# Expert rows and activations transposed by VectorE in blocks of 32, weights stored in the order of the chunks, rows gathered a quarter per partition

## The chip, the cores and the metric

The kernel runs on one core of one Trainium2 chip. The metric is the device time of one execution in microseconds (us). Five engines work beside each other, each through its own list of instructions in order: TensorE (PE; PEld is its loading of weights), VectorE (DVE), ScalarE (ACT), GpSimd (POOL) and SyncE (SP, which here only issues transfers). Sixteen DMA engines move data between the memory (HBM) and the on-chip buffer (SBUF, 128 partitions); they are fed by queues, q1 for the transfers that SP issues and q0 for those of POOL. Products end in PSUM, eight banks.

## The reference

512 tokens of 1024 features pass through two blocks. Block 1: a norm, a mixer of pools and attention, an output product, a residual, and then a layer of 32 experts of which each token takes four:

```python
def moe(h, w_router, b_router, w_gate_up, b_gate_up, w_down, b_down):
    logits = (ht @ w_router + b_router).astype(jnp.float32)
    top_vals, top_idx = lax.top_k(logits, TOP_K)           # 4 of 32
    gates = jax.nn.softmax(top_vals, axis=-1)
    ...
    def expert_block(args):
        xblk, e = args
        gu = xblk @ w_gate_up[e] + b_gate_up[e]             # 1024 x 2048
        gate = jnp.minimum(gu[:, :D_EXPERT], SWIGLU_LIMIT)
        up = jnp.clip(gu[:, D_EXPERT:], -SWIGLU_LIMIT, SWIGLU_LIMIT)
        act = gate * jax.nn.sigmoid(SWIGLU_ALPHA * gate) * (up + 1)
        return act @ w_down[e] + b_down[e]                  # 1024 x 1024
    ...
    y = jnp.zeros((T + 1, D), h.dtype).at[row_tok].add(row_gate[:, None].astype(h.dtype) * yb)
```

Block 2 holds a gated delta rule beside a sparse attention, an output product, a norm and a gate. All is computed in float32. The 32 experts hold 12.58 MB of weights each, 403 MB in all.

## The kernel before

**Stages.** Block 1 up to the router takes about the first 240 us, the experts run to about 1306 us, block 2 from there to the end. Only the experts and the seams on both sides are touched.

**The stream of weights.** An expert is six chunks of 2 MB: four of gate and up (256 rows of the contraction each, `load_q`, line 382) and two of down (512 rows each, line 388). A chunk lies in SBUF as 128 partitions of 16 KB. Of gate and up a partition gets two rows of 8 KB, of down four rows of 4 KB. The 192 chunks go in one order into a ring of slots (nine in steady use, `PAT`); SP issues a chunk as soon as the products that read its slot are done (`more`). Chunks 7 to 9 are issued on POOL's queue. SP also loads the biases (`bias`, lines 1115 and 1116).

**The order of the experts.** After the first two they run by a plan by rank of load: `expert_plan` gives each of the 32 places room for 2, 3 or 4 groups of 32 rows, 86 groups together. Which expert stands at a place is known only at run time (`perm`). Rows beyond the room are done in a loop at the end, which has no turns here.

**One expert, in the order of the code** (the loop over `i`). Gate and up: for each of eight steps `kc` of the contraction and each group four products (`gate_up`, L1140), each of 32 rows against 128 x 512 weights, into a bank of PSUM. Beside them the next experts are made ready:

- `prep_a(i + 2)`: products with a one-hot matrix give the token numbers, gates and rates of the rows (L416, L417); then POOL gathers the rows from `h_rows` (`gather`, L404), whole rows of 4 KB, one row per partition, 64 to 128 rows.
- `prep_r(i + 2)`: one product (L441) brings token numbers, gates and rates into the layout of the products (`iy`, `gt`, `rs`).
- `prep_b(i + 1)`: eight transposes by TensorE (L1128, tile `pht`) and two products by VectorE out of PSUM with the gain of the norm (L1129) make `hT`, the rows by feature; a shuffle spreads the biases (L1133).

Then for each group `act` on VectorE and ScalarE (L1146 to L1154), `act_t` with two transposes by TensorE (L1160, tile `pat`) and a copy by ScalarE (L1162), and `down` with 32 products (L1171), the bias and the gate on VectorE (L1176, L1177) and a scatter by POOL that adds the rows to `y_rows` (L1179), 128 rows of 1 KB. The transposes of the last group stand inside the down products of the group before it, since the in-order TensorE would wait for `act` otherwise.

**The seams.** For expert 0 the token numbers come by a path of their own (`place_0`, `rows_0`, L1040, then L1057 and one gather), so that its first product can start early. At the last expert POOL issues the first weights of block 2 (`load_w2`, L454, L455 and L463), and its last down chunk comes in two halves.

Of the kernel before, what the change touches and what calls it, by code (L numbers as in the profile page):

```python
# [24 lines left out]
# ---------------------------------------------------------------- packed columns  # L25
# [10 lines left out]
for _n, _w in (("ident", 128), ("g_attn", 8), ("tri", 128), ("cmask", 128), ("iota", 128), ("invrow", 16), ("invcol", 1),  # L36
               ("sgncol", 1), ("poolfix", 64), ("pcol", 1), ("pcol4", 1), ("jcol", 1), ("dumr", 1), ("sel", 128), ("grp", 4), ("kadd", 1), ("caps", 32), ("eye4", 32),
               ("g_q_a", 2), ("g_kv_a", 1), ("b_pool", 4), ("pool_scale", 4),
               ("g_out_pool", 4), ("g_out_attn", 4), ("g_ffn", 8), ("c", 8), ("b_ada", 16), ("g_pre", 8)):
    _col(_n, _w)  # L40
# [77 lines left out]

def layout(inputs):
# [10 lines left out]
    pk["g_ffn"] = col(f("g_ffn_norm"))  # L130
    pk["c"] = col(f("c_2"))
# [3 lines left out]
    for n, (o, w) in _COLS.items():  # L135
# [45 lines left out]
        "w_gu": f("w_gate_up")[0],  # L181
        "w_dn": f("w_down")[0],
# [15 lines left out]
def expert_plan():  # L198
    """Order in which the experts run (by rank of load; ranks 0 and 1 are experts 0 and 1) and groups of 32 rows for each."""
# [14 lines left out]
class Model:  # L214
    """When the engines, each in its order, would be through with the instructions given so far (in us)."""
# [75 lines left out]
def build(tc, ia, out, dbg=None):  # L291
# [12 lines left out]
    with ctx:  # L304
# [10 lines left out]
        hdram = nc.dram_tensor("h_rows", (513, 1024), F32).ap()  # L315
# [27 lines left out]
        # ============================================================ block 1, before the experts  # L343
# [10 lines left out]
        ig0 = mid.tile([128, 1], I32, name="ig0")  # L354
# [4 lines left out]
        # ---- expert weights: one stream of chunks over the rings  # L359
# [19 lines left out]
        def load_q(i, q, e, key, eng=S):  # L379
            w = rings[key].tile([128, 4096], F32, name="ew", tag=key)  # L380
            if q < 4:
                eng.dma_start(w.rearrange("p (k n) -> p k n", k=2),
                            ia["w_gu"][e, 256 * q:256 * q + 256, :].rearrange("o (k p) n -> p (o k) n", p=128))
            else:
                # the very last one in two, so that half of it is used while the other comes
                m = 2 if (i, q) == chunks[-1] else 4
                for k in range(0, 4, m):
                    r = 512 * (q - 4) + 128 * k
                    eng.dma_start(w.rearrange("p (k n) -> p k n", k=4)[:, k:k + m],
                                  ia["w_dn"][e, r:r + 128 * m, :].rearrange("o (k p) n -> p (o k) n", p=128))  # L390
            loaded[i, q] = w

        # ---- rows of the experts
# [42 lines left out]
        def prep_r(i, bank):  # L436
            """Rows, gates and rates in the layout of the products."""
# [6 lines left out]
            V.tensor_scalar(iy[:, :ng], pv[:, :, 0], C("jcol"), None, op0=add)  # L444
            V.tensor_copy(gt[:, :ng], pv[:, :, 1])
# [19 lines left out]
        with tc.tile_pool(name="t1", bufs=1) as tp, tc.tile_pool(name="ps1", bufs=1, space=PSUM) as ps:  # L465
# [5 lines left out]
            # ---- loads, in the order of their use  # L471
# [52 lines left out]
            # ---- rms norm of x, transposed  # L524
# [15 lines left out]
            # ---- latent projections by tokens  # L540
# [27 lines left out]
            # ---- rope tables; those of the queries carry the scale of the scores  # L568
# [51 lines left out]
            # ---- rel_bias of block 2 by distance: row 128 h + 127 - q has the distances of the query q, descending  # L620
# [11 lines left out]
            # ---- pool mixer, a group at a time  # L632
# [48 lines left out]
            # ---- modulation sums  # L681
# [34 lines left out]
            def mod_cols(q):  # L716
                """Shift and scale, by rows."""
# [24 lines left out]
            # ---- heads  # L742
# [19 lines left out]
            # ---- attention  # L762
# [55 lines left out]
            # ---- order of the work  # L818
# [9 lines left out]
            S.dma_start(hdram[512:513].rearrange("o (p n) -> (o p) n", p=128), zt[:, :8])  # L828
# [100 lines left out]
            # ---- output projection, residual, router  # L929
# [99 lines left out]
            oh0 = tp.tile([128, 4, 128], BF, name="oh0")  # L1029
            pk = [pmm(), pmm(), pmm()]  # L1030

            def place_0(t):
                """The rows of expert 0 in a tile, by their place: the first expert wins a tie, so its mask is a comparison."""
                src = pk[t // 3][:, t % 3:t % 3 + 1]
                V.tensor_scalar(oh0[:, t, :n0], C("iota")[:, :n0], src, m0f[:, t:t + 1], op0=ALU.is_equal, op1=mul)
# [21 lines left out]
            V.tensor_scalar(ig0[:n0], pk[2][:n0, :1], 2048.0, 0.25, op0=add, op1=mul)  # L1057
# [8 lines left out]
            # the rates of the rows in three exact parts  # L1066
# [12 lines left out]
        # ============================================================ experts  # L1079
        with tc.tile_pool(name="mo", bufs=1) as mp, \  # L1080
# [13 lines left out]
            bank = lambda name: ps.tile([128, 512], F32, name=name, tag="a", bufs=5)  # L1094
            bank2 = lambda name: ps.tile([128, 512], F32, name=name, tag="b", bufs=2)

            # the slot of the first chunk, in pieces of the tiles of the products
# [21 lines left out]
            def prep_b(i, hf):  # L1119
                """The rows, transposed; the biases, in all rows."""  # L1120
                st = ST[i]
                n = st["n"]
                if hf == 0:
                    st["hT"] = mp.tile([128, 8, 128], F32, name="hT2", bufs=2)
                p = bank2("pht").rearrange("p (c n) -> p c n", c=4)
# [1074 lines left out]
```

## Time and profile before

| | |
|---|---|
| median of 3 runs | 1701.57 us (1700.75 to 1701.81) |
| the profiled execution: its span, first to last instruction | 1702.8 us |
| TensorE busy | 1583.6 us, 93% |
| VectorE busy | 813.9 us, 48% |
| ScalarE busy | 322.7 us, 19% |
| POOL busy | 285.2 us, 17% |
| moved by DMA | 489.86 MB, mean 288 GB/s |

The profile gives no time for its execution other than the span; the span is 1.2 us above the median of the runs. "Busy" is the time in which an engine executes something; on TensorE it holds a slower clock and the small gaps inside a run of products as well. A DMA share is the mean over 16 engines of the time in which packets were under way; at the edges of packets it counts a little twice, so that it can pass 1. "Landing" is the time from a transfer's issue to its end. In names, `ew` is a chunk of the experts' weights, `hg` the gathered rows, `hT` the transposed rows, `pgu` and `pdn` the sums of gate and up and of down, `zt` a piece of one slot that holds the activations and the results, `cpk` the packed constants.

### The profile page before, as it was taken

The numbers are of one execution on the slowest core, as the hardware profiler recorded it, in microseconds if no ns is written. First come the engines' busy times: TensorE is split into PE (matmuls) and PEld (weight loads), VectorE is DVE, ScalarE is ACT, GpSimd is POOL, SyncE is SP. The second block draws the span as 40 slices with busy tenths as digits, with TensorE's granted clock in tenths as the row PEclk, the third lists the DMA queues.
The fourth block names the chain that finished last, engine by engine and source line by source line (L and its number), as shares of the span: only waits on it lengthen the run. The fifth ranks groups of instructions, "written<-read, shape, count | busy, mean of one in ns | idle before, by whom it ended". The sixth has DMA issues, their size and how long they took to land. (4 is left out here: it accounts for less than half of the span.)

```text
span 1702.8 us, 36458 instructions
## 1 busy us (share of the span) xinstructions
PE 1583.6 (93%) x15401; PEld 783.9 (46%) x15403; DVE 813.9 (48%) x2243; ACT 322.7 (19%) x793; POOL 285.2 (17%) x304
## 2 busy tenths in 40 slices
PE   9789989999999999889999998999995899988998
PEld 5345443433343343333433433433342767766856
DVE  5965245434334343333343333333432676868744
ACT  3145120000000000000000000000001755443342
POOL 1820011112121112111211211212111101011121
PEclk9989989999999999999999999999998899999999
DMA  8536658999999999999999999999995421121002
GB/s 337 187 132 194 256 233 304 360 400 365 402 388 398 396 394 394 397 404 393 387 395 401 393 387 407 400 390 380 401 400 201 169 80 57 54 77 58 39 1 99
DMA packets 100041, 489.86 MB, mean 288 GB/s; under 512 B 7860, under 2 KB 20660, under 8 KB 65444
## 3 DMA queue, kind: packets, MB, share of 16 engines
q1 hardware_dynamic: 81572, 455.98, 68.1%
q0 software_dynamic: 17296, 28.91, 7.1%
q8 instruction: 122, 2.00, 0.5%
q10 hardware_dynamic: 1008, 2.62, 0.4%
q14 instruction: 43, 0.35, 0.1%
HBM read 469.13 MB, written 21.24 MB: 288 GB/s over the span
## 5 line engine op out<-in xcount | busy, mean ns | idle before, releaser
L1140 PE MATMUL pgu<-ew,hT 128*32 128x512 f32 x5504 | 643.8, 604 | 9.9 <-DMA ew<-in_w_gu 7.1
L1171 PE MATMUL pdn<-ew,zt 128*32 128x256 f32 x5504 | 311.2, 381 | 4.4 <-SPq L1355 3.5
L1140 PEld LDWEIGHTS pgu<-ew,hT 128*32 128x32 f32 x5504 | 162.1, 111 | 327.1 <-issue 295.5
L1179 POOL DMA_INDIRECT y_rows<-zt,iy x86 | 135.2, 1572 | 766.2 <-DVE zt L1177 710.0
L1171 PEld LDWEIGHTS pdn<-ew,zt 128*32 128x32 f32 x5504 | 175.8, 110 | 136.4 <-issue 22.1
L1150 ACT ACTIVATE sg<-zt 128x256 f32<-128x256 f32 x86 | 35.9, 417 | 793.6 <-DVE zt L1148 793.4
L1176 DVE TENSOR_TENSOR zt<-pdn,bb 128x256 f32<-128x256 f32 x86 | 36.5, 425 | 209.0 <-PE pdn L1171 209.0
L1146 DVE SCALAR_TENSOR_TENSOR zt<-pgu,rs,bb 128x512 f32<-128x512 f32 x86 | 64.4, 749 | 118.1 <-PE pgu L1140 118.1
L286 PE MATMUL pmm<-h2h,wx 128*128 128x512 f32 x320 | 109.5, 404 | 1.0 <-ACT qbT L286 1.0
L1129 DVE TENSOR_TENSOR hT<-pht,cpk 128x256 f32<-128x256 f32 (+2 forms) x64 | 33.0, 516 | 132.7 <-PE pht L1128 132.6
L286 PEld LDWEIGHTS pmm<-h2h,wx 128*128 128x128 f32 x320 | 60.0, 187 | 20.6 <-issue 6.5
L1162 ACT ACTIVATE zt<-pat 128x256 f32<-128x256 f32 x86 | 32.9, 383 | 191.8 <-PE pat L1160 191.8
L286 PE MATMUL pmm<-h2l,wx 128*128 128x512 f32 x160 | 62.4, 390 | 1.1 <-DVE h2l L286 1.1
L1160 PE MATMUL pat<-cpk,zt 128*128 128x128 f32 x172 | 37.4, 299 | 23.4 <-DVE zt L1154 23.2
L811 PE MATMUL pmm<-wo,mix 128*128 128x512 f32 x128 | 56.5, 595 | 0.0
L1160 PEld LDWEIGHTS pat<-cpk,zt 128*128 128x128 f32 x172 | 17.4, 142 | 83.5 <-issue 56.6
L404 POOL DMA_INDIRECT hg<-h_rows,ig x32 | 32.7, 1023 | 135.2 <-issue 107.8
L420 DVE COPY sl<-pix 64x9 f32<-64x9 f32 (+2 forms) x32 | 5.2, 163 | 103.1 <-PE pix L417 103.1
L1128 PEld LDWEIGHTS pht<-cpk,hg 64*128 64x128 f32 (+2 forms) x256 | 23.1, 142 | 52.3 <-issue 52.3
L1154 DVE TENSOR_TENSOR zt<-zt,sg 128x256 f32<-128x256 f32 x86 | 36.6, 425 | 9.3 <-DVE zt L1152 0.5
L769 PE MATMUL pmm<-KT,qT 128*128 128x128 f32 (+3 forms) x64 | 25.1, 476 | 14.0 <-ACT pe L777 13.5
L1152 DVE SCALAR_TENSOR_TENSOR zt<-zt 128x256 f32<-128x256 f32 x86 | 36.6, 425 | 3.0
(511 smaller groups left out, 1976.6 us busy)
## 6 DMA issues: line engine op xcount, KB each, us to landing
ew<-in_w_gu SPq DMA_DIRECT2D x125, 2048.0 KB, 26.1
ew<-in_w_dn SPq DMA_DIRECT2D x63, 2048.0 KB, 32.5
w<-in_w SPq DMA_DIRECT2D x8, 2048.0 KB, 7.9
ada<-in_w_ada SPq DMA_DIRECT2D x12, 512.0 KB, 4.3
qT<-in_w_ada SPq DMA_DIRECT2D x12, 512.0 KB, 4.1
ew<-in_w_gu POOLq DMA_DIRECT2D x3, 2048.0 KB, 13.8
wo<-in_w_out SPq DMA_DIRECT2D x2, 2048.0 KB
wina<-in_w_in_a SPq DMA_DIRECT2D x1, 2048.0 KB, 15.0
```

What stands on the lines that cost most here:

```text
L286: return f(*args, **kw)
L811: T.matmul(pp[hf], mix[0][:, 4 * part + c, 128 * t:128 * t + 128], wout[part][:, c, 512 * hf:512 * hf + 512], start=c == 0, stop=c == 3)
L1129: V.tensor_tensor(st["hT"][:, 4 * hf:4 * hf + 4, :n], p[:, :, :n], C("g_ffn")[:, 4 * hf:4 * hf + 4, None].to_broadcast([128, 4, n]), op=mul)
L1140: T.matmul(p[32 * j:32 * j + 32], st["hT"][:, kc, 32 * g:32 * g + 32], w[:, kc % 2, :, j], start=kc == 0 if first is None else first, stop ...
L1146: V.scalar_tensor_tensor(gu, p.rearrange("p (h m) -> p h m", h=2), st["rs"][:, g:g + 1], st["bb"][:, 0:2], op0=mul, op1=add)
L1150: A.activation(sg, gu[:, 0], AF.Sigmoid, scale=1.702)
L1152: V.scalar_tensor_tensor(gu[:, 1], gu[:, 1], 1.0, gu[:, 0], op0=add, op1=mul)
L1154: V.tensor_tensor(a, gu[:, 1], sg, op=mul)
L1160: T.transpose(p[:, h], a[:, 128 * h:128 * h + 128], ident)
L1171: T.matmul(p[32 * j:32 * j + 32], aT[:, c % 2, 32 * f:32 * f + 32], w[:, c % 4, j], start=c == 0, stop=c == 7)
L1176: V.tensor_tensor(y, p, st["bb"][:, 2], op=add)
L1179: d = G.indirect_dma_start(out=ydram, out_offset=bass.IndirectOffsetOnAxis(ap=st["iy"][:, g:g + 1], axis=0), in_=y, in_offset=None, comput ...
```

## The change

Five things change, all in the experts' stage.

1. The weights are one tensor `w_e`, ordered before the launch so that each chunk is 128 partitions of 16 KB without a break. The last chunk still comes in two halves, 8 KB per partition each. `load_q` is one transfer.
2. The rows are gathered as quarter rows: `h_rows` is seen as 2048 rows of 256, and a group of 32 rows is one gather in which partition 32 j + r gets quarter j of row r (1 KB). There is one gather per group, issued in `prep_r`; rows that hold nothing have a number beyond the bound and are left out. Before there was one per expert, issued in `prep_a`.
3. The rows are transposed by VectorE in blocks of 32 x 32 (`rows_t`), followed by the product with the gain (`g_ffnq`), per group. The order of the contraction differs from before, and the order of the weights follows it.
4. The activations are transposed by VectorE at the end of `act`; `act_t` is gone and the down products of a group are no longer split around it.
5. Expert 0's start: the one-hot matrix is repeated for the four quarters and three groups, with 24 small products instead of 8 and three gathers instead of one. The transposes' two banks of PSUM go to the others, seven of one kind.

```diff
@@ chunked
+def chunked(gu, dn):
+    gu = gu.reshape(32, 4, 4, 2, 32, 2048).transpose(0, 2, 1, 4, 3, 5).reshape(32, 4, 128, 4096)
+    dn = dn.reshape(32, 4, 2, 4, 32, 1024).transpose(0, 2, 1, 4, 3, 5).reshape(32, 2, 128, 4096)
+    return np.concatenate([gu, dn], 1)
@@ load_q
-            if q < 4:
-                eng.dma_start(w.rearrange("p (k n) -> p k n", k=2),
-                            ia["w_gu"][e, 256 * q:256 * q + 256, :].rearrange("o (k p) n -> p (o k) n", p=128))
-            else:
-                m = 2 if (i, q) == chunks[-1] else 4
-                for k in range(0, 4, m):
-                    r = 512 * (q - 4) + 128 * k
-                    eng.dma_start(w.rearrange("p (k n) -> p k n", k=4)[:, k:k + m],
-                                  ia["w_dn"][e, r:r + 128 * m, :].rearrange("o (k p) n -> p (o k) n", p=128))
+            m = 2048 if (i, q) == chunks[-1] else 4096
+            for o in range(0, 4096, m):
+                eng.dma_start(w[:, o:o + m], ia["w_e"][e, q, :, o:o + m].rearrange("o p n -> p (o n)"))
@@ gather
-        def gather(n, turn, ig):
-            G.indirect_dma_start(out=hgs[turn % 2][:n], out_offset=None, in_=hdram,
-                                 in_offset=bass.IndirectOffsetOnAxis(ap=ig, axis=0),
-                                 bounds_check=511, oob_is_err=False)
+        def gather(turn, g, ig):
+            G.indirect_dma_start(out=hgs[turn % 2][:, 256 * g:256 * g + 256], out_offset=None, in_=hquart,
+                                 in_offset=bass.IndirectOffsetOnAxis(ap=ig[:, g:g + 1], axis=0),
+                                 bounds_check=2047, oob_is_err=False)
@@ rows_of
-            if i:
-                ig = pool.tile([128, 1], I32, name="ig", bufs=2)
-                V.tensor_scalar(ig[:n], rw[:n, 3:4], 2048.0, 0.25, op0=add, op1=mul)
-                gather(n, turn, ig[:n, :1])
@@ prep_r
             V.tensor_scalar(iy[:, :ng], pv[:, :, 0], C("jcol"), None, op0=add)
+            if i:
+                for g in range(ng):
+                    gather(st["turn"], g, iy)
@@ rows_0
-                    for k in range(2):
-                        T.matmul(pk[2][:n0, :1], oh0[:, t, :n0], R[:, t, 0, k:k + 1], start=t == 0 and k == 0,
-                                 stop=t == 3 and k == 1)
+                    for g in range(3):
+                        for k in range(2):
+                            T.matmul(pk[2][:, g:g + 1], oh0[:, t, g].rearrange("p j r -> p (j r)"), R[:, t, 0, k:k + 1],
+                                     start=t == 0 and g == 0 and k == 0, stop=t == 3 and k == 1, skip_group_check=True)
...
-            gather(n0, 0, ig0[:n0, :1])
+            for g in range(3):
+                gather(0, g, ig0)
@@ prep_b becomes rows_t and biases
-                for c in range(4):
-                    c8 = 4 * hf + c
-                    T.transpose(p[:, c, :n], st["hg"][:n, 128 * c8:128 * c8 + 128], ident[:n, :n])
-                V.tensor_tensor(st["hT"][:, 4 * hf:4 * hf + 4, :n], p[:, :, :n],
-                                C("g_ffn")[:, 4 * hf:4 * hf + 4, None].to_broadcast([128, 4, n]), op=mul)
+                for g in range(st["ng"]):
+                    o = st["hT"][:, g]
+                    V.transpose(o.rearrange("p c r -> p (c r)"), st["hg"][:, 256 * g:256 * g + 256])
+                    V.tensor_tensor(o, o, gain.to_broadcast([128, 8, 32]), op=mul)
@@ act, act_t
-                return a
-            def act_t(a):
-                p = bank2("pat")[:, :256].rearrange("p (h n) -> p h n", h=2)
-                for h in range(2):
-                    T.transpose(p[:, h], a[:, 128 * h:128 * h + 128], ident)
-                aT = slot("aT").rearrange("p (h n) -> p h n", h=2)
-                A.activation(aT, p, AF.Copy)
-                return aT
+                aT = slot("aT")
+                V.transpose(aT, a)
+                return aT
@@ the loop over the experts
                     for g in range(ng):
-                        last = g == ng - 2
-                        down(i, g, aTs[g], p_ := bank("pdn")[:, :256], range(5))
-                        if last:
-                            aTs.append(act_t(acts[-1]))
-                        down(i, g, aTs[g], p_, range(5, 8))
+                        down(i, g, aTs[g], bank("pdn")[:, :256], range(8))
```

On TensorE, an expert of two groups in the middle of the stage stands like this before (from its product for `prep_r` to the first products of the next expert, where `pht` are row transposes and `pat` activation transposes):

```order
997 L441 MATMUL pix<-rx,cpk 128x12
998 L1140 MATMUL pgu<-ew,hT_7615 32x512 x8
999 L1128 MATMUL pht<-cpk,hg_102 128x96 x4
1000 L1140 MATMUL pgu<-ew,hT_7615 32x512 x8
1001 L1128 MATMUL pht<-cpk,hg_102 128x96 x4
1002 L1140 MATMUL pgu<-ew,hT_7615 32x512 x20
1003 L1160 MATMUL pat<-cpk,zt 128x128 x2
1004 L1140 MATMUL pgu<-ew,hT_7615 32x512 x4
1005 L1171 MATMUL pdn<-ew,zt 32x256 x20
1006 L1160 MATMUL pat<-cpk,zt 128x128 x2
1007 L1171 MATMUL pdn<-ew,zt 32x256 x44
1008 L1140 MATMUL pgu<-ew,hT_7981 32x512 x24
```

and this after:

```order
831 L1142 MATMUL pgu<-ew,hT_7408 32x512 x8
832 L440 MATMUL pix<-rx,cpk 128x12
833 L1142 MATMUL pgu<-ew,hT_7408 32x512 x40
834 L1166 MATMUL pdn<-ew,zt 32x256 x64
835 L1142 MATMUL pgu<-ew,hT_7755 32x512 x24
```

The four rows of transposes are gone; the 40 products of gate and up and the 64 of down stand without a break.

On VectorE the same expert, from the copies of `prep_r` to the activation of its first group, before:

```order
1057 L444 TENSOR_SCALAR iy_107<-pix,cpk 128x2
1058 L445 COPY gt_111<-pix 128x2
1059 L446 COPY rs_115<-pix 128x2
1060 L1129 TENSOR_TENSOR hT_7981<-pht,cpk 128x4x96 x2
1061 L1133 STREAM_SHUFFLE bb<-bsrc 128x768
1062 L1146 SCALAR_TENSOR_TENSOR zt<-pgu,rs_113,bb 128x512
```

and after, where `STREAM_TRANSPOSE` is the transpose in blocks of 32:

```order
1192 L448 COPY rs_115<-pix 128x2
1193 L1129 STREAM_TRANSPOSE hT_7755<-hg_102 128x256
1194 L1130 TENSOR_TENSOR hT_7755<-hT_7755,cpk 128x256
1195 L1129 STREAM_TRANSPOSE hT_7755<-hg_102 128x256
1196 L1130 TENSOR_TENSOR hT_7755<-hT_7755,cpk 128x256
1197 L1129 STREAM_TRANSPOSE hT_7755<-hg_102 128x256
1198 L1130 TENSOR_TENSOR hT_7755<-hT_7755,cpk 128x256
1199 L1135 STREAM_SHUFFLE bb<-bsrc 128x768
1200 L1148 SCALAR_TENSOR_TENSOR zt<-pgu,rs_113,bb 128x512
```

The three groups of the next expert are transposed there in six instructions that read the gathered rows themselves; VectorE's own queue now waits for the gather, where TensorE's did before, and the activations stand behind it.

On POOL, the gathers of an expert and the scatters of the one before it, before:

```order
76 L1178 MEMSET spacer 1x1
77 L1179 DMA y_rows<-zt,iy_107 2560x256
78 L404 DMA hg_102<-h_rows,ig 128x1024
79 L1178 MEMSET spacer 1x1
80 L1179 DMA y_rows<-zt,iy_104 2560x256
```

and after:

```order
76 L1173 MEMSET spacer 1x1
77 L1174 DMA y_rows<-zt,iy_107 2560x256
78 L407 DMA hg_102<-h_rows,iy_106 128x256 x4
79 L1173 MEMSET spacer 1x1
80 L1174 DMA y_rows<-zt,iy_104 2560x256
```

One gather of 128 rows has become four of 128 quarter rows, at the same place between the scatters.

## Rows read from the trace of the kernel before

**Rows 1.** The page's head.
```profile
span 1702.8 us, 36458 instructions
```

**Rows 2.** Windows: length, PE PEld DVE ACT POOL busy, PEclk, DMA share, GB/s.
```profile
310.00:650.00 340.00, 332.07 (x3902) 131.37 (x3898) 133.90 (x443) 21.99 (x55) 59.90 (x71) 0.99 1.03 391
650.00:1000.00 350.00, 334.69 (x3822) 129.73 (x3818) 134.78 (x433) 23.21 (x58) 54.11 (x64) 0.98 1.03 395
1000.00:1290.00 290.00, 272.60 (x3196) 107.86 (x3192) 106.62 (x345) 17.61 (x44) 48.85 (x58) 0.99 1.03 395
```

**Rows 3.** Waits of PE, 310 to 1290 us: total us, times, longest.
```profile
PE pgu L1140 <- DMA ew<-in_w_gu: 7.1, 3, 3.3
```

**Rows 4.** Timeline of PE: start, us, line, operation, [idle before].
```profile
714.76 7.42 PE L1140 MATMUL pgu<-ew,hT 128*32 128x512 f32 x40 [3.31 <-DMA ew<-in_w_gu]
```

**Rows 5.** DMA, 310 to 1290 us: packets, MB, share; issues, us to landing.
```profile
q1 hardware_dynamic: 62552, 364.47, 92.7%
q0 software_dynamic: 14907, 19.49, 9.5%
...
ew<-in_w_gu SPq DMA_DIRECT2D x115, 2048.0 KB, 26.1
...
w<-in_w POOLq DMA_DIRECT2D x1, 832.0 KB, 11.3
```

**Rows 6.** DMA, 369 to 377 us: packets and q1.
```profile
DMA packets 818, 3.22 MB, mean 403 GB/s; under 512 B 25, under 2 KB 37, under 8 KB 817
...
q1 hardware_dynamic: 817, 3.21, 101.4%
```

**Rows 7.** DMA, 555 to 567 us: packets and q1.
```profile
DMA packets 655, 5.05 MB, mean 421 GB/s; under 512 B 40, under 2 KB 40, under 8 KB 40
...
q1 hardware_dynamic: 654, 5.03, 100.9%
```

**Rows 8.** DMA, 88 to 97 us (weights of block 1): packets and q1.
```profile
DMA packets 306, 3.97 MB, mean 441 GB/s; under 512 B 32, under 2 KB 32, under 8 KB 74
...
q1 hardware_dynamic: 306, 3.97, 103.3%
```

**Rows 9.** DMA, 484.7 to 488.2 us: q1 and q0.
```profile
q1 hardware_dynamic: 143, 1.13, 80.2%
q0 software_dynamic: 137, 0.13, 23.2%
```

**Rows 10.** The page's groups: busy us, mean ns | idle before, releaser.
```profile
L1176 DVE TENSOR_TENSOR zt<-pdn,bb 128x256 f32<-128x256 f32 x86 | 36.5, 425 | 209.0 <-PE pdn L1171 209.0
...
L1129 DVE TENSOR_TENSOR hT<-pht,cpk 128x256 f32<-128x256 f32 (+2 forms) x64 | 33.0, 516 | 132.7 <-PE pht L1128 132.6
...
L1162 ACT ACTIVATE zt<-pat 128x256 f32<-128x256 f32 x86 | 32.9, 383 | 191.8 <-PE pat L1160 191.8
...
L1160 PE MATMUL pat<-cpk,zt 128*128 128x128 f32 x172 | 37.4, 299 | 23.4 <-DVE zt L1154 23.2
...
L404 POOL DMA_INDIRECT hg<-h_rows,ig x32 | 32.7, 1023 | 135.2 <-issue 107.8
```

**Rows 11.** Timeline of PE at the start of the experts.
```profile
232.05 0.89 PE L1040 MATMUL pmm<-R,oh 128*96 128x1 bf16 x8
...
238.34 1.51 PE L1128 MATMUL pht<-cpk,hg 96*128 96x96 f32 x8 [1.08 <-DMA hg<-h_rows,ig]
...
240.02 3.29 PE L1140 MATMUL pgu<-ew,hT 128*32 128x512 f32 x16 [0.16 <-issue]
```

**Rows 12.** Windows in the first experts, columns as in rows 2.
```profile
255.00:265.00 10.00, 9.39 (x93) 3.40 (x88) 6.22 (x41) 0.00 (x0) 1.63 (x3) 1.00 0.44 149
...
275.00:280.00 5.00, 4.68 (x88) 2.88 (x92) 0.78 (x2) 0.27 (x1) 0.00 (x0) 1.00 0.61 179
```

**Rows 13.** Timeline of PE at the end of the experts.
```profile
1296.36 3.64 PE L1171 MATMUL pdn<-ew,zt 128*32 128x256 f32 x32 [3.49 <-SPq L1355]
...
1301.10 5.39 PE L1171 MATMUL pdn<-ew,zt 128*32 128x256 f32 x96 [0.47 <-ACT zt L1162]
```

More of the change, by code (lines that the diff above doesn't have):

```diff
@@ L130, in layout @@
     pk["g_ffn"] = col(f("g_ffn_norm"))
+    pk["g_ffnq"] = f("g_ffn_norm").reshape(4, 8, 32).transpose(0, 2, 1).reshape(128, 8)
     pk["c"] = col(f("c_2"))
@@ L180, in layout @@
         "w_ada": f("w_ada_2")[0],
-        "w_gu": f("w_gate_up")[0],
-        "w_dn": f("w_down")[0],
+        "w_e": chunked(f("w_gate_up")[0], f("w_down")[0]),
         "b_gu": f("b_gate_up")[0],
@@ L313, in build @@
         ctx.enter_context(tc.manual_schedule())
-        hdram = nc.dram_tensor("h_rows", (513, 1024), F32).ap()
+        hquart = nc.dram_tensor("h_rows", (2048, 256), F32).ap()
+        hdram = hquart.rearrange("(t j) n -> t (j n)", j=4)
         ydram = nc.dram_tensor("y_rows", (4 * (512 + 128), 256), F32).ap()
@@ L353, in build @@
         gd = mid.tile([128, 4, 32], F32, name="gd")
-        ig0 = mid.tile([128, 1], I32, name="ig0")
+        ig0 = mid.tile([128, 3], I32, name="ig0")
         key = mid.tile([32, 1], F32, name="key")
@@ L1117, in bias, with rows_t, biases @@
                 BS[i] = r
-            def prep_b(i, hf):
+            def rows_t(i):
                 st = ST[i]
[L1122 to L1125, printed above, removed]
-                for c in range(4):
-                    c8 = 4 * hf + c
-                    T.transpose(p[:, c, :n], st["hg"][:n, 128 * c8:128 * c8 + 128], ident[:n, :n])
-                V.tensor_tensor(st["hT"][:, 4 * hf:4 * hf + 4, :n], p[:, :, :n],
-                                C("g_ffn")[:, 4 * hf:4 * hf + 4, None].to_broadcast([128, 4, n]), op=mul)
-                if hf:
-                    st["bb"] = mp.tile([128, 3, 256], F32, name="bb", bufs=2)
-                    V.stream_shuffle(st["bb"].rearrange("p h m -> p (h m)"), bsrc.rearrange("p h m -> p (h m)"),
-                                     [BS.pop(i)] * 32)
+                st["hT"] = mp.tile([128, 4, 8, 32], F32, name="hT2", bufs=2)
+                gain = C("g_ffnq")[:, :, None]
+                for g in range(st["ng"]):
+                    o = st["hT"][:, g]
+                    V.transpose(o.rearrange("p c r -> p (c r)"), st["hg"][:, 256 * g:256 * g + 256])
+                    V.tensor_tensor(o, o, gain.to_broadcast([128, 8, 32]), op=mul)
+            def biases(i):
+                ST[i]["bb"] = mp.tile([128, 3, 256], F32, name="bb", bufs=2)
+                V.stream_shuffle(ST[i]["bb"].rearrange("p h m -> p (h m)"), bsrc.rearrange("p h m -> p (h m)"),
+                                 [BS.pop(i)] * 32)
             def gate_up(i, g, kc, p, first=None):
@@ L1272, in build @@
             gates()
-            prep_b(0, 0)
-            prep_b(0, 1)
+            rows_t(0)
+            biases(0)
             beside = {
@@ L1305, in build @@
                     elif i and kc == 3 and i + 1 < NEXP:
-                        prep_b(i + 1, 0)
+                        rows_t(i + 1)
                 if i == 0:
@@ L1309, in build @@
                 more(6 * i + 11)
-                acts, aTs = [], []
+                aTs = []
                 seq = [(g, h) for g in range(ng) for h in range(2)]
@@ L1321, in build @@
                         if kc == 5 and g == 0 and 0 < i < NEXP - 1:
-                            prep_b(i + 1, 1)
+                            biases(i + 1)
                             if i + 2 < NEXP:
                                 bias(i + 2)
-                        if kc == (7 if edge else 6) and g:
-                            aTs.append(act_t(acts[g - 1]))
                     if i == 0:
@@ L1329, in build @@
                     if h:
-                        acts.append(act(i, g, pg[g]))
+                        aTs.append(act(i, g, pg[g]))
                 more(6 * i + 13)
@@ L1333, in build @@
                     prep_r(2, pix)
-                    prep_b(1, 0)
-                    prep_b(1, 1)
+                    rows_t(1)
+                    biases(1)
                 if edge:
@@ L1339, in build @@
                         for g in range(ng):
-                            if h == 0 and g == ng - 1:
-                                aTs.append(act_t(acts[-1]))
                             down(i, g, aTs[g], ps_[g], cs)
@@ L1387, in build @@
                 bias("o")
-                prep_b("o", 0)
-                prep_b("o", 1)
+                rows_t("o")
+                biases("o")
                 pg = bank("pgu")
@@ L1395, in build @@
                         gate_up("o", 0, 2 * q + 1, pg)
-                down("o", 0, act_t(act("o", 0, pg)), bank("pdn")[:, :256], range(8))
+                down("o", 0, act("o", 0, pg), bank("pdn")[:, :256], range(8))
                 V.tensor_scalar(EE, EE, -32.0, None, op0=add)
```

19 lines of the change are left out of this document (8 added, 11 removed).

## The prediction

> **What bounds the kernel now.** I read the page's head first: the span is 1702.8 us [rows 1]. Then the busy times by stage. In three stretches of the experts TensorE is busy 332 of 340, 335 of 350 and 273 of 290 us, so it looks like the bound, but the DMA share is 1.03 in each at 391 to 395 GB/s [rows 2]. Two views decide between them. TensorE waits for weights: between 310 and 1290 us three times, 7.1 us in all [rows 3], and the row at 714.76 shows what follows such a wait, 40 products of gate and up in 7.42 us [rows 4]. The DMA view of the same 980 us shows the other side: a chunk of 2 MB lands a median 26.1 us after its issue [rows 5], while at 421 GB/s [rows 7] it moves in 5 us. So about five chunks are always queued; the DMA engines never run dry, and a chunk is late because the stream is slow, not because it was asked for late. The weights' queue (q1) moved 364.47 MB there, 92.7% of the engines; an expert is 12.58 MB, so 29.0 experts at 33.8 us each. POOL's software queue (q0: gathers, scatters) has 14907 packets and 9.5%. Work taken from TensorE inside this stage buys nothing while the stream stays full; what a packet costs is worth 31 times what it is worth once.
>
> **Part 1: longer packets.** Per DMA engine an expert's gate and up chunks are 4 x 16 packets of 8 KB now and its down chunks 2 x 32 of 4 KB, 128 in all; afterwards 6 x 8 of 16 KB, 48. What a packet costs beside its bytes comes from two windows in which q1 had the engines to itself. 369 to 377 us, down chunks: 817 packets, 37 of them under 2 KB, so 780 of 4 KB in 16 x 8 = 128 engine-us, 164.1 ns each [rows 6]. 555 to 567 us, gate and up: 654, 40 of them small, so 614 of 8 KB in 192 us, 312.7 ns [rows 7]. Four KB more cost 148.6 ns, so 164.1 - 148.6 = 15.5 ns would be fixed if the small packets cost nothing. At the 95 ns of a small packet of q0 (23.2% x 16 x 3.5 us / 137, [rows 9]) they leave 159.6 and 306.5 ns, and 12.7 ns are fixed. For 16 KB this gives about 610 ns; the one stretch of before with such packets (another load, 88 to 97 us) has 306 packets, 74 of them under 8 KB: 144 / 232 = at most 621 ns [rows 8], by which a step from 8 to 16 KB saves only 2 x 312.7 - 621 = 4 ns. I take 11, somewhat under the value of the two windows of this very stream, for the third; the ends are 4 and 15.5. So 80 packets fewer x 11 ns = 0.88 us an expert, x 31 (the first chunks arrive before the stage is full) = -27.3 us (-10 to -38).
>
> The Trainium skill has its own price for this ("DMA: Bandwidth & Descriptors", "Why small descriptors are slow"): about three bus cycles a packet on top of one per 32 B. By that page an 8 KB packet loses 1.2%, a 4 KB one 2.3%, a 16 KB one 0.6%, and this term would be about -9 us, an estimate. The rows' 36 ns per KB put a cycle at 1.2 ns, and 12.7 ns are nearer to ten cycles than to three.
>
> **Part 2: gathers of quarter rows.** The 2048 rows come as four packets of 1 KB instead of one of 4 KB: 2048 x 3 / 16 = 384 packets more per engine, x 11 ns = +4.2 us (+1.5 to +6). Issuing goes from 32 gathers of 1.02 us on POOL [rows 10] to 86, +55 us over a stage in which POOL is busy 163 of 980 us [rows 2]: hidden, unless its queue fills (rival D). The gather is now issued behind prep_r's copy, some microseconds later, and is used an expert later; covered by 30 us. Stream together: -23.1 us (-8 to -32).
>
> **Part 3: transposes.** TensorE loses 172 activation transposes of 299 ns, 37.4 us, the 23.2 us of waiting before them, and 256 row transposes; ScalarE loses 86 copies, 32.9 us [rows 10]. Between 310 and 1290 us this is worth nothing, the stream covers it; TensorE only waits longer for chunks. VectorE gains per group two transposes of 128x256 and one product of that size, and loses the 33.0 us out of PSUM. No transpose stands in the trace; the nearest rows of the size are the sum out of PSUM, 425 ns, and ScalarE's copy, 383 [rows 10]. I take 0.43 us (0.38 to 0.52, the product L1129): 86 x 3 x 0.43 - 33 = +78 us. VectorE was busy 134 of 340 us and 135 of 350 [rows 2]; it goes to some 47%. The activation of a group is ready 0.43 us later, against a copy and a TensorE transpose that go; where a down product of another group stands between (two groups at least), nobody waits. Without that cover it would cost 86 x 0.43 = 37 us, and the full queue of chunks takes up such a delay too.
>
> **Part 4: start.** Expert 0's addresses take 24 products instead of 8 (0.89 us for 8): +1.8 us. The first group's gather then lands as before, its VectorE transpose and product (0.86 us) replace eight TensorE transposes (1.51 us) and a product, and the two further gathers are 2 us behind. The first product of the experts stands 1.7 us after the first row transpose; it comes 1 to 3 us later [rows 11]. Against it: the DMA is at 0.44 and 0.61 in 255 to 265 and 275 to 280 us, 7.6 us idle, since chunks wait for slots that TensorE frees [rows 12], and expert 0's and expert 1's products lose some 2.5 us of transposes each (three groups x two x 299 ns and the rows'). Net -1 (-5 to +3).
>
> **Part 5: end.** The last expert ends on TensorE with nothing above it: products at 1296.36 for 3.64 us, then the transposes and the copy, then the last at 1301.10 [rows 13]: 1301.10 - 1300.00 = 1.1 us go. Before that TensorE waits 3.49 us for the last chunk, which shares the engines with block 2's loads on POOL's queue (11.3 us to land for the first, [rows 5]). Those have the right to one packet for each of q1's; with half to a quarter of q1's packets fewer of them come between. 16 packets an engine at 95 ns are 1.5 us; I take 2 (0 to 4). End -3 (-1 to -5).
>
> **Sum.** -23 - 1 - 3 = -27: the profiled 1702.8 becomes 1675.8. The median of the runs is 1.2 us below the span, so about 1675; the likeliest case's own range is 1660 to 1692.
>
> **Rivals.** B: longer packets bring nothing, since the rate is set elsewhere (memory), or since the hardware cuts them. For it: 16 KB at 621 ns is within 1% of twice 8 KB [rows 8]. Against it: 4 KB and 8 KB differ by 403 to 421 GB/s [rows 6, 7]. Then +4 - 1 - 2 = +1: about 1702. Chance 0.14.
>
> C: more than the forecast, a fixed cost of 15.5 ns and a start that gains 5: below 1660. Chance 0.06.
>
> D, slower: POOL's software queue becomes the bound. Where both queues have work they take turns packet by packet: in 484.7 to 488.2 us q1 had 143 and q0 137 packets [rows 9]. A packet of q0 then costs itself and one of q1, 95 + 312 ns before, 95 + 610 after; a gather or scatter of 8 per engine 5.6 us, and 86 / 32 = 2.69 groups with one of each 30.4 us an expert, beside 33.0 of the stream. It decides from 33 us on: if each gather, waiting behind scatters, adds one or two landings of 2 us, it is 34.4, x 31 = +43 us on the forecast, 1718. For it: the gather's rows are used in the next expert, and VectorE stands still behind them with the activations. Against it: before, a gather carried four times the bytes per packet in one transfer, and half the packets of 128 place rows beyond a group's are dropped. Chance 0.08. The Trainium skill ("DMA: Bandwidth & Descriptors", the passage on arbitration between the queues) lets an engine drain 9 to 17 descriptors of one queue before it turns to the other; by that a small transfer would wait far longer and D would be likelier, but 143 to 137 in this trace is one for one.
>
> **How the numbers follow.** Forecast 0.72, B 0.14, C 0.06, D 0.08. The range for 8 in 10 leaves out D, the upper half of B and the edge of C: 1660 to 1699. What a measurement of this kernel tells from no change is 0.2%, 3.4 us. Faster by more: the forecast, C and a little of B, 0.83; within: the rest of B, 0.09; slower: 0.08.
>
> **What would show it.** Right: q1's packets fall from 62552 to some 24000 in such a window, the fourfold share of packets under 2 KB, a rate near 400 GB/s or above with the DMA share still about 1.03, some 33.0 us an expert, longer TensorE waits for chunks, no transposes on TensorE, VectorE's near 0.43 us, the last product some 27 us earlier. Wrong: an unchanged GB/s at full share (B); a DMA share under 1 in the middle with VectorE waiting for gathers at the row transposes, and landings of q0 of 20 us and more (D).

## The result and the profile after

The changed kernel takes 1659.48 us (median of four runs, 1653.45 to 1661.73) against 1701.16 us, a ratio of 0.9747 with a 95% interval of 0.9728 to 0.9765: 42 us less, where 27 were forecast. The direction was right, the size too small, and 1659.5 lies just outside the range of 1660 to 1699. The profiled execution's span is 1659.5 us, 43.3 below the one before. Of all runs behind this document one, of the first experiment, took 1847 us, 9% more than its fellows, and is left out of its ratio as slow.

The stages first. These are the windows of the changed kernel that answer to [rows 2] (columns as there; the experts end earlier, so the last one is shorter):

```profile
310.00:650.00 340.00, 326.75 (x4006) 130.79 (x4002) 163.26 (x522) 12.52 (x30) 80.22 (x90) 0.99 1.02 409
650.00:1000.00 350.00, 320.41 (x3738) 122.12 (x3733) 157.30 (x509) 12.09 (x29) 77.33 (x86) 0.96 1.02 411
1000.00:1250.00 250.00, 231.81 (x2714) 88.76 (x2710) 104.98 (x337) 7.92 (x19) 53.97 (x61) 0.97 1.01 406
```

The DMA engines are still full (1.01 to 1.02), but they move 406 to 411 GB/s instead of 391 to 395. TensorE is busy 92 to 96% instead of 94 to 98, VectorE 42 to 48% instead of 37 to 39. TensorE's waits in 310 to 1240 us (total us, times, longest) answer to [rows 3]:

```profile
PE pgu L1142 <- DMA ew<-in_w_e: 35.5, 16, 4.0
PE pdn L1166 <- DVE zt L1158: 12.6, 8, 3.1
PE pdn L1166 <- DMA ew<-in_w_e: 5.1, 11, 1.2
```

It now waits 40.6 us for chunks in place of 7.1: the stream is clearly the slower of the two. The DMA view of the same stretch, 930 us (packets, MB, share), against [rows 5]:

```profile
q1 hardware_dynamic: 25400, 361.44, 92.4%
q0 software_dynamic: 15221, 18.04, 9.2%
```

The weights come in 14.2 KB a packet on the mean, and 361.44 / 12.58 = 28.7 experts in 930 us are 32.4 us each, against 33.8. That is 1.4 us an expert where -0.88 + 0.14 = -0.74 were forecast, and 31 x 0.7 = 21 us of difference, an estimate from this one execution; the medians are 15 us off the forecast. The software queue did not grow to four packets a row: 15221 packets in 930 us against 14907 in 980.

The groups of the changed kernel (busy us, mean ns | idle before) show the new operations:

```profile
L407 POOL DMA_INDIRECT hg<-h_rows,iy x83 | 86.4, 1041 | 211.7 <-DVE rs L448 176.8
...
L1158 DVE STREAM_TRANSPOSE zt<-zt 128x256 f32<-128x256 f32 x86 | 38.3, 446 | 3.0
...
L1130 DVE TENSOR_TENSOR hT<-hT,cpk 128x256 f32<-128x256 f32 x86 | 36.6, 425 | 3.0
...
L1129 DVE STREAM_TRANSPOSE hT<-hg 128x256 f32<-128x256 f32 x86 | 37.5, 436 | 0.1
```

A transpose of 128x256 in blocks of 32 takes 436 to 446 ns (0.43 was taken), a gather of a group 1.04 us on POOL.

At the end of the experts (timeline of TensorE), against [rows 13]:

```profile
1252.60 1.93 PE L1166 MATMUL pdn<-ew,zt 128*32 128x256 f32 x32 [1.20 <-DVE zt L1158]
1255.27 3.66 PE L1166 MATMUL pdn<-ew,zt 128*32 128x256 f32 x64 [0.74 <-DVE zt L1158]
1259.52 1.93 PE L1166 MATMUL pdn<-ew,zt 128*32 128x256 f32 x32 [0.59 <-SPq L1342]
```

The last product ends at 1261.45 instead of 1301.10 + 5.39 = 1306.49, 45.0 us earlier; what follows took 398.0 us instead of 396.3. So the whole gain lies in the experts, and the question is what made it half as large again as forecast.

### The profile page after: what moved, and what is told of

It is laid out like the page before. It is cut to its first block, busy times and chain, and to the rows that moved or that the text cites. A ratio compares the mean times of both kernels' runs of the same rounds, so it can differ in the third digit from the quotient of the medians.

```text
span 1659.5 us, 35749 instructions
## 1 busy us (share of the span) xinstructions
PE 1519.4 (92%) x14991; PEld 756.6 (46%) x14991; DVE 872.2 (53%) x2406; ACT 289.4 (17%) x707; POOL 343.1 (21%) x358
## 5 line engine op out<-in xcount | busy, mean ns | idle before, releaser
L1142 PE MATMUL pgu<-ew,hT 128*32 128x512 f32 x5504 | 632.2, 608 | 40.9 <-DMA ew<-in_w_e 35.5
L1142 PEld LDWEIGHTS pgu<-ew,hT 128*32 128x32 f32 x5504 | 173.7, 112 | 422.6 <-issue 354.1
L407 POOL DMA_INDIRECT hg<-h_rows,iy x83 | 86.4, 1041 | 211.7 <-DVE rs L448 176.8
L1158 DVE STREAM_TRANSPOSE zt<-zt 128x256 f32<-128x256 f32 x86 | 38.3, 446 | 3.0
L818 DVE SCALAR_TENSOR_TENSOR x1b<-pmm,rpo,x1b 128x512 f32<-128x512 f32 x16 | 12.0, 751 | 50.9 <-PE pmm L813 50.2
L1130 DVE TENSOR_TENSOR hT<-hT,cpk 128x256 f32<-128x256 f32 x86 | 36.6, 425 | 3.0
L1129 DVE STREAM_TRANSPOSE hT<-hg 128x256 f32<-128x256 f32 x86 | 37.5, 436 | 0.1
L813 PEld LDWEIGHTS pmm<-wo,mix 128*128 128x128 f32 x128 | 24.4, 195 | 28.6 <-issue 28.1
```

What stands on the lines that cost most here:

```text
L407: G.indirect_dma_start(out=hgs[turn % 2][:, 256 * g:256 * g + 256], out_offset=None, in_=hquart, in_offset=bass.IndirectOffsetOnAxis(ap=ig ...
L813: T.matmul(pp[hf], mix[0][:, 4 * part + c, 128 * t:128 * t + 128], wout[part][:, c, 512 * hf:512 * hf + 512], start=c == 0, stop=c == 3)
L1129: V.transpose(o.rearrange("p c r -> p (c r)"), st["hg"][:, 256 * g:256 * g + 256])
L1130: V.tensor_tensor(o, o, gain.to_broadcast([128, 8, 32]), op=mul)
L1142: T.matmul(p[32 * j:32 * j + 32], st["hT"][:, g, kc], w[:, kc % 2, :, j], start=kc == 0 if first is None else first, stop=kc == 7)
L1158: V.transpose(aT, a)
```

## The experiments

Each run is given as its ratio to runs of the kernel before on the same chip, with a 95% interval; 0.001 is 1.7 us. Three theories stood at first. **1**: the packets cost about what was forecast, and a second saving was missed: gathers that cover 64 or 96 of the 128 partitions slow the weights' packets beside them, and the new ones, which cover all 128, do not. **2**: the packets alone did it, at a higher fixed price. **3**: the transposes that left TensorE free the slots sooner.

What led to theory 1 are windows of before around two gathers of whole rows. This is the gather of an expert of two groups (64 partitions), 421.4 to 424.0 us; rows: packets in all, then q1 and q0 with packets, MB, share:

```profile
DMA packets 162, 0.81 MB, mean 310 GB/s; under 512 B 39, under 2 KB 39, under 8 KB 88
...
q1 hardware_dynamic: 84, 0.61, 78.5%
q0 software_dynamic: 78, 0.20, 24.9%
```

and this one of an expert of four groups (128 partitions), 397.0 to 401.9 us:

```profile
DMA packets 367, 2.09 MB, mean 426 GB/s; under 512 B 54, under 2 KB 55, under 8 KB 170
...
q1 hardware_dynamic: 213, 1.61, 77.9%
q0 software_dynamic: 154, 0.47, 23.9%
```

The engines are as full in both, but beside the 64 rows they move 310 GB/s, beside the 115 rows 426. A MB of q1 took 0.785 x 16 x 2.6 / 0.61 = 53.5 engine-us (us of one of the 16 DMA engines) in the first and 0.779 x 16 x 4.9 / 1.61 = 37.9 in the second. Beside a gather over 96 partitions, 491.8 to 496.4 us, q1 has this row, 0.752 x 16 x 4.6 / 1.16 = 47.7 engine-us a MB:

```profile
q1 hardware_dynamic: 153, 1.16, 75.2%
```

The single packets of the trace say the same of all gathers between 310 and 1230 us that have 8 KB packets beside them: beside the 22 over 64 or 96 partitions such a packet took 370 to 444 ns (the mean at each gather), beside the five over 128 partitions 309 to 339.

**The gather's list over all partitions, nothing else.** Rows past the group's room get a number beyond the bound; the same rows move in packets of the same size.

```diff
                 ig = pool.tile([128, 1], I32, name="ig", bufs=2)
+                V.memset(ig, 4096)
                 V.tensor_scalar(ig[:n], rw[:n, 3:4], 2048.0, 0.25, op0=add, op1=mul)
-                gather(n, turn, ig[:n, :1])
+                gather(128, turn, ig[:, :1])
```

> The kernel before, with the gather's list of rows filled up to 128 partitions with numbers beyond the bound, so that the same rows move in the same packets but the list covers all partitions. Theory 1 (a gather that covers 64 or 96 partitions slows the weights' packets beside it, one that covers 128 does not; summed over the trace of before, the packets near such gathers lose 16 us): 1685, 14 to 17 us less than before, and weights' packets near a gather at 310 to 320 ns instead of 390 to 420. Theory 2 (the longer packets alone made the gain, at a fixed price of nearer 18 ns): 1701, no change. Theory 3 (the transposes taken from TensorE free slots sooner): 1701, no change.

Measured: 0.9938 (0.9916 to 0.9959), 7 to 14 us less: the direction of theory 1 alone, though hardly its 14 to 17 us. The gather of the same expert in this kernel, 420.4 to 423.7 us:

```profile
DMA packets 299, 1.39 MB, mean 421 GB/s; under 512 B 104, under 2 KB 104, under 8 KB 155
...
q1 hardware_dynamic: 157, 1.18, 84.5%
q0 software_dynamic: 142, 0.21, 16.9%
```

A MB of q1 takes 0.845 x 16 x 3.3 / 1.18 = 37.8 engine-us, as beside 128 partitions. The contention is shown, and it was in the kernel before in most of its gathers (26 of the 32 experts have room for two or three groups). What in the chip makes it, no run shows. The numbers beyond the bound still leave packets, but small ones: 104 under 512 B here. In 310 to 1230 us the weights gained 348.20 against 343.14 MB, 13.6 us of stream, and about 10 arrived in the time.

**Packets of 16 KB alone.** Weights stored chunk by chunk in the old order of the contraction; gathers and transposes as before.

```diff
+def chunked(gu, dn):
+    gu = gu.reshape(32, 4, 2, 128, 2048).transpose(0, 1, 3, 2, 4).reshape(32, 4, 128, 4096)
+    dn = dn.reshape(32, 2, 4, 128, 1024).transpose(0, 1, 3, 2, 4).reshape(32, 2, 128, 4096)
...
+                eng.dma_start(w[:, o:o + m], ia["w_e"][e, q, :, o:o + m].rearrange("o p n -> p (o n)"))
```

> The kernel before with its weights stored in the order of the chunks, 16 KB per partition without a break; gathers and transposes as before. Theory 1 with a price of 9 to 11 ns a packet: 22 to 27 us less than before, 1674 to 1679. Theory 2: 40 us less or more, 1655 to 1662. Theory 3: 11 ns a packet, as theory 1.

Measured: 0.9906 (0.9882 to 0.9929), 16 us less. Less than any theory gave: theory 2 falls, and theory 1's 22 to 27 us are missed too. The short gathers still stand in this kernel, and the longer packets meet them as well. Beside the same gather (423.8 to 427.0 us) q1 takes 0.854 x 16 x 3.2 / 0.82 = 53.3 engine-us a MB:

```profile
q1 hardware_dynamic: 64, 0.82, 85.4%
```

**Both edits**, transposes still on TensorE.

> The kernel before with both edits: chunks of 16 KB per partition and the list of rows over 128 partitions; transposes still on TensorE. Theories 1 and 2: within 5 us of the changed kernel, 1655 to 1664. Theory 3: 1674 or more, since the transposes are still on TensorE.

Measured: 0.9806 (0.9779 to 0.9833), 33 us less. That is more than the two alone (10 + 16), though the three intervals, 4 to 5 us each, allow the plain sum. It is still 10 to 13 us from the changed kernel, which repeated beside other runs came to 0.9728 (0.9701 to 0.9755). The expectation of theories 1 and 2 missed by 8 us; theory 3 had 1674 or more, and the median is 1671.86. TensorE's waits in this kernel, 310 to 1230 us, point at the reason:

```profile
PE pat L1159 <- DVE zt L1153: 9.8, 17, 4.4
PE pix L440 <- DVE rx L432: 8.5, 12, 0.7
PE pix L440 <- PE pgu L1139: 1.4, 2, 0.7
```

No wait for a chunk is left, and its window of 920 us shows TensorE at 98% and the DMA share at 1.01:

```profile
310.00:1230.00 920.00, 900.34 (x10573) 356.13 (x10566) 369.43 (x1232) 61.20 (x153) 157.71 (x186) 1.00 1.01 406
```

So a theory **3b**: with the faster stream, TensorE with its transposes becomes the bound.

**Old packets in the changed kernel.** The same layout cut again into 8 KB for gate and up and 4 KB for down.

```diff
+    cut = lambda a, k: a.reshape(32, -1, 128, k, 4096 // k).transpose(0, 1, 3, 2, 4).reshape(32, -1, 524288)
+    return np.concatenate([cut(gu, 2), cut(dn, 4)], 1)
...
+                eng.dma_start(w.rearrange("p (k n) -> p k n", k=k)[:, o:o + m],
+                              ia["w_e"][e, q, 128 * n * o:128 * n * (o + m)].rearrange("o (k p n) -> p (o k) n", p=128, n=n))
```

> The changed kernel with its weights stored so that packets are as before, 8 KB for gate and up and 4 KB for down. Theory 1: 80 packets an expert more at 9 to 11 ns, 1682 to 1687. Theory 2: all of the gain goes, 1700. Theory 3: 1685.

Measured: 0.9886 (0.9862 to 0.9910), a median of 1682.55, as theory 1 had it (theory 3's 1685 is as near). The step to 16 KB is worth 0.9886 - 0.9728 = 0.0158, 27 us here. Gathers, transposes and the new start without it already bring 19.

**Four needless products an expert**, in three kernels: with the transposes gone, with both edits and the transposes, and before. The edit is one line:

```diff
                         if 0 < i < NEXP - 2:
+                            warm(pix().rearrange("p (a n) -> p a n", a=4), 4)
                             prep_a(i + 2, mp, pix)
```

> The changed kernel once more, beside the other runs of this call: 0.973 to 0.977 of the time before, so that the kernel with both edits on the old transposes (0.981) can be set against it on the same footing.

> The changed kernel with four needless products of 128x512 (bf16, about 0.23 us each) for each of 29 experts on TensorE, ahead of prep_a: 27 us of work in all. Theory 3b (the stream, once faster, is no longer the cover of the old transposes; TensorE has become the bound where they are kept, and not where they are gone): 0 to 8 us more than the changed kernel. Rival (the stream of weights bounds all of them): 0.

> The kernel before with chunks of 16 KB and gathers over 128 partitions (transposes on TensorE), with the same four needless products an expert, 27 us in all. Theory 3b: 18 to 27 us more than without them (1672), 1690 to 1699. Rival (the stream bounds it, and the 12 us to the changed kernel come from the start, the end or the form of the gathers): 0 to 5 us more.

> The kernel before with the same four needless products an expert on TensorE, 27 us in all, nothing else changed. Theory 3b in its strong form (TensorE stood just under the stream in the kernel before already, with 40.6 us idle between 310 and 1290 us that lie in short waits): 8 to 20 us more, 1711 to 1723. As the prediction had it (the stream covers TensorE): 0 to 4 us more.

Measured: the changed kernel 0.9744 (0.9711 to 0.9776) with them, 0.9728 without: 3 us. With both edits and the old transposes 0.9955 (0.9941 to 0.9970) against 0.9806: 25 us of the 27. Before: 1.0019 (1.0005 to 1.0033), 3 us. Theory 3b holds in its weak form alone: before, the stream covered TensorE, as the prediction had it; with the faster stream and the old transposes it no longer does, and without them it does again. The window of the kernel before, without and with the needless products:

```profile
310.00:1230.00 920.00, 883.36 (x10260) 347.02 (x10256) 356.01 (x1164) 59.00 (x148) 151.97 (x180) 0.99 1.03 393
310.00:1230.00 920.00, 901.05 (x10352) 355.91 (x10348) 354.18 (x1158) 58.87 (x147) 152.09 (x180) 1.00 1.03 393
```

TensorE's busy time rose by 17.7 us and the rate stayed. The same window of the kernel with both edits and the needless products:

```profile
310.00:1230.00 920.00, 903.39 (x10400) 356.85 (x10396) 358.15 (x1193) 59.23 (x148) 153.07 (x180) 1.00 1.00 400
```

and of the changed kernel, without and with them:

```profile
310.00:1230.00 920.00, 862.13 (x10324) 336.91 (x10320) 425.27 (x1366) 32.53 (x78) 207.03 (x232) 0.98 1.02 410
310.00:1230.00 920.00, 875.41 (x10448) 347.46 (x10444) 426.22 (x1366) 32.52 (x78) 208.04 (x233) 0.99 1.02 410
```

With both edits TensorE, at 900 of 920 us already, took in only 3 us more, the DMA share sank by 0.01 and the rate from 406 to 400 GB/s. In the changed kernel TensorE took the extra work into its waits, and the rate stayed; its waits for chunks are 22.5 us there, where they were 40.6:

```profile
PE pgu L1142 <- DMA ew<-in_w_e: 14.5, 10, 3.7
PE pdn L1166 <- DMA ew<-in_w_e: 8.0, 6, 2.1
```

**All packets of 4 KB in the changed kernel**, the edit above with 4 and 4 in place of 2 and 4.

> The changed kernel with all of its weights in packets of 4 KB: 192 packets an expert and engine instead of 48. At the 9.3 ns that the step from 48 to 128 packets cost (1682.6 against 1659.5 us), 144 x 9.3 ns x 31 = 41 us more than the changed kernel, 1695 to 1702. If the price were one of the down chunks' shape and not of the packet's number: about 1682.

Measured: 0.9980 (0.9961 to 0.9999). Against the changed kernel 0.0252, 43 us for 144 packets an expert: 9.6 ns a packet over 31 experts. From 48 to 128 packets it is 10.8 ns, from 128 to 192 8.1, the same within the intervals (5 to 6 us on either step are some 2.5 ns). The price goes by the number of packets.

**Scatters of real rows alone.** The scatter writes all 128 quarter rows of a group, also those that hold nothing.

```diff
-                                         in_=y, in_offset=None, compute_op=add)
+                                         in_=y, in_offset=None, compute_op=add,
+                                         bounds_check=2047, oob_is_err=False)
```

> The changed kernel with a bound on the scatters' row numbers, so that the rows of a group that hold nothing are left out of the scatter instead of being written to rows that nobody reads. 86 x 128 - 8192 = 2816 packets of 1 KB fewer at 101 ns of one of 16 engines: 17.8 us of the stream. If the stream bounds the changed kernel: 13 to 18 us less, 1642 to 1646. If TensorE or POOL's queue bounds it: 0 to 5 us less.

Measured: 0.9708 (0.9682 to 0.9734), 3 us less than 0.9728, within the intervals of both, where 13 to 18 were expected of a kernel that the stream bounds; a miss. Its DMA rows for 310 to 1230 us:

```profile
q1 hardware_dynamic: 25445, 361.87, 93.4%
q0 software_dynamic: 15122, 15.41, 7.8%
```

The changed kernel has there 358.16 MB and 17.62 MB. So 2.2 MB of empty rows did go, and the weights moved 1.0% more, some 9.5 us of stream. The packets did not become fewer, 15122 against 14928: a row that is left out still leaves a small packet (under 512 B there are 8420 against 5967). The last expert product ends at 1254.49 instead of 1261.45, 7 us earlier, and the rest of the program took longer, 400.3 us against 398.0, and 394.2 in the repeated changed kernel. A rest that differs by 6 us from one execution to the next can hide a good part of the gain. That some engines keep more of the full rows than others and set the pace is another guess at the part that is missing; no view here names the engine of a packet, and it stays open.

**Biases on ScalarE's queue**, alone and with the bound on the scatters.

```diff
-                e = bass.ds(regs["o"], 1) if i == "o" else which(i)
-                S.dma_start(bsrc[r:128:32, 0:2], ia["b_gu"][e, :].rearrange("o (h j m) -> (o j) h m", h=2, j=4))
-                S.dma_start(bsrc[r:128:32, 2], ia["b_dn"][e, :].rearrange("o (j m) -> (o j) m", j=4))
+                eng = S if i == "o" else A
+                e = bass.ds(regs["o"], 1) if i == "o" else which(i, eng)
+                eng.dma_start(bsrc[r:128:32, 0:2], ia["b_gu"][e, :].rearrange("o (h j m) -> (o j) h m", h=2, j=4))
+                eng.dma_start(bsrc[r:128:32, 2], ia["b_dn"][e, :].rearrange("o (j m) -> (o j) m", j=4))
```

> The changed kernel with the biases' loads issued by ScalarE in place of SP, so that they do not queue behind five chunks. VectorE waits 146 us for them in the changed kernel, TensorE 15 to 23 us for activations behind that. If the stream alone bounds it: 0 to 2 us less. If TensorE's waits for activations still count: 5 to 12 us less, with those waits under 5 us.

> The changed kernel with the bound on the scatters and the biases on ScalarE's queue. If the two add: 1646 to 1652; if the biases bring nothing: 1654.

Measured: alone 0.9736 (0.9714 to 0.9758), no change. VectorE waited for the biases like this in the changed kernel, 310 to 1230 us:

```profile
DVE bb L1135 <- DMA bsrc<-in_b_dn: 146.2, 21, 11.9
```

This wait is gone, TensorE's waits for activations behind it are down to 0.8 us, and TensorE waits for chunks instead, 53.8 us against 40.6:

```profile
PE pgu L1143 <- DMA ew<-in_w_e: 38.7, 16, 3.7
PE pdn L1167 <- DMA ew<-in_w_e: 15.1, 8, 3.3
```

The stream bounds the changed kernel. Both together: 0.9694 (0.9673 to 0.9716), 1650.97 us, the best version, 6 to 9 us under the changed kernel. That lies in the range for "the two add", although the biases alone brought nothing; the intervals don't separate it from the 3 us of the bound alone.

## Why the prediction was wrong

**What bounds the kernel** was read rightly: needless work on TensorE cost the kernel before 3 us of 27, and the stream's rate set the gain.

**Part 1, packets: right.** Forecast 27.3 us at 11 ns a packet; in the changed kernel these 80 packets an expert measured 27 us (10.8 ns), and by the 9.6 ns of the whole step from 192 to 48 packets they are 24 us. The Trainium skill's rule ("DMA: Bandwidth & Descriptors", "Why small descriptors are slow"), three bus cycles a packet, would have given 9 us, an estimate; at the 1.2 ns a cycle of the prediction the runs measure about eight such cycles. A slip of the working, on which only rival D rests: the 610 ns for a packet of 16 KB go with a fixed price of 15.5 ns; with 12.7 ns they are 600.

**Part 2, gathers: the step that failed first.** The prediction said "the 2048 rows come as four packets of 1 KB instead of one of 4 KB", +4.2 us. Neither half held. The quarter rows travel several to a packet: the DMA view of the changed kernel around one gather, 411.2 to 417.0 us, has 161 - 110 = 51 packets between 2 and 8 KB, where quarters that moved one by one would all be under 2 KB:

```profile
DMA packets 293, 2.40 MB, mean 414 GB/s; under 512 B 69, under 2 KB 110, under 8 KB 161
...
q1 hardware_dynamic: 148, 2.15, 87.7%
```

Over 310 to 1230 us it has 18219 - 16431 = 1788 such packets, and the kernel with both edits, which gathers whole rows, 18449 - 16681 = 1768. Some packets of the trace have 1036, 2056 or 3076 bytes, that is one, two or three quarter rows and 4 bytes for each that was left out; so a packet holds four entries of the list, of different rows, since all four quarters of a row are kept or left out together.

And a MB of q1 takes 0.877 x 16 x 5.8 / 2.15 = 37.9 engine-us beside it: the slowing by gathers over 64 or 96 partitions is gone with them. That saving, 10 us in the kernel before and 17 beside the longer packets (0.9906 to 0.9806), was in none of the terms; with the +4.2 us that did not come, this is the larger part of the miss. It could have been seen, since the two windows from which the packets' price was taken were chosen for having no gather in them; a third one beside a gather shows 310 GB/s. [Rows 9], the window with both queues at work, held scatters and was read for the turns alone.

**Part 3, transposes: the step that failed second.** "Between 310 and 1290 us this is worth nothing, the stream covers it" was true of the stream before, not of the one that parts 1 and 2 leave. With both edits and the old transposes the kernel stands at 0.9806, without them at 0.9728 to 0.9747: 10 to 13 us. Start, end and the finer gathers are in that difference too, and no run takes the transposes away alone; but between 310 and 1230 us the changed kernel moved 358.16 MB of q1 against 354.92, 8.4 us of stream, so most of it came in the middle, where the needless products show TensorE as the bound. The prediction noted TensorE's 94 to 98% and did not ask how far the stream could shrink before TensorE was next. It was idle 980 - 939.4 = 40.6 us between 310 and 1290 us [rows 2], and not all of that can be filled, since part of it are waits for VectorE. What the longer packets gave by kernel fits this: 16 us beside the old gathers and the transposes, 22 with the gather's list filled (0.9938 to 0.9806), 27 in the changed kernel, though each has 4 to 6 us of interval.

**Parts 4 and 5.** The first expert product came 0.85 us later, where 1 to 3 were forecast:

```profile
240.87 3.75 PE L1142 MATMUL pgu<-ew,hT 128*32 128x512 f32 x24 [0.46 <-DVE hT L1130]
```

The DMA share of 240 to 310 us rose from 0.87 to 0.95. At the end the 1.1 us between the last down products are 0.59 us of waiting for a chunk now. Their -4 us together is not separated by any run.

**The rivals.** B fell (the packets brought 16 to 27 us), D fell (q1 and POOL's queue had 148 and 144 packets beside the gather shown, still one for one, and the rate rose), C, "below 1660", came out by its number and for a wrong reason: the price is 9.6 ns and not 15.5.

## What to carry to other kernels

When a stage is bound by one resource and another is busy 95% or more beside it, work out both after the change: once the cover shrinks, the covered work counts. Here the edits worth 10 and 16 us alone brought 33 together, and the transposes, which the old stream covered, some 10 more. Beside the clean stretch that gives a transfer's price, look at one with the disturbance that the stage really has; here the difference was a saving of its own. Here an indirect gather was better spread over all 128 partitions, if only by filling up its list with numbers beyond the bound (10 us).

## What the runs showed of the hardware

- Beside a gather of 4 KB rows whose list covers 64 partitions the weights' packets took 53.5 engine-us a MB, beside one over 96 partitions 47.7, beside one over 128 partitions 37.9; the 64 with a list filled up to 128, of which the last were left out by the bound, took 37.8.
- The packets' fixed price was 9.6 ns (8 to 11 by step) between 4 and 16 KB.
- An indirect gather of 1 KB quarter rows over 128 partitions went in packets of up to 4 KB, four entries of the list each, and the queue's packets did not grow fourfold (15221 in 930 us against 14907 in 980).
- An entry beyond the bound still left a packet under 512 B: with 2.2 MB of rows left out of the scatters the queue had 15122 packets against 14928.
- A transpose of 128x256 float32 in blocks of 32 on VectorE takes 436 ns from the gathered rows and 446 from the activations.
